# The two ends of a planned decoder kernel: another order of the first transfers and passes, small matmuls ahead of the data, and a last layer norm in 512-column pieces on VectorE

## The chip, the cores and the metric

The kernel runs on one core of a Trainium2 chip. Its time is what the device needs for one execution, in microseconds (us); the time before is the median of three executions, 1533.29 us (1532.67 to 1533.56). One further execution was taken with the hardware profiler. All rows of a profile or a trace in this text come from that one.

## The reference, cut to what matters

Two layers of a decoder trunk are computed for 512 tokens of width 1024. In each, one projection of the residual stream feeds four branches (a recurrent mixer, latent attention, a convolution, cross-attention into a memory); their outputs are merged with gates, projected once more and added to the stream, which is then normalised over its 1024 channels:

```python
for l in range(DEPTH):                       # 2
    h = x @ w_in[l]                          # cut into the inputs of all branches
    ...                                      # four branches: y_rwkv, y_mla, y_conv, y_mem
    proj = jnp.einsum('bsnc,ncd->bsnd', branches, w_o_branch[l])
    gates = jax.nn.sigmoid(merge.reshape(B, S, N_BRANCH, D) + b_gate[l])
    out = jnp.sum(gates * proj, axis=2) @ w_out[l]
    x = _layer_norm(DEEPNORM_ALPHA * x + out, ln_g[l], ln_b[l])
```

The layer norm takes mean and variance of a token's 1024 values, subtracts the one, multiplies by the reciprocal root of the other, multiplies by `ln_g` and adds `ln_b`.

## The kernel before, in words

**Arithmetic.** Every fp32 matmul is made of three passes. An operand a is split in a rounded part (called h, a cast on ScalarE) and the rest (called lo or l, a subtraction on VectorE); `mm3` then issues three matmuls: h of the left with lo of the right, h with h, lo with h. All of them go through one helper (line 322 of the profile), and every vector operation through another (line 242), so the profile tells them apart by tile names alone.

**Order.** No engine's order is left to a compiler. A planner (`Plan`) keeps a modelled clock for each engine and a modelled transfer queue, and the kernel is written as Python generators that are resumed at modelled times. Each instruction takes its place in its engine's program when its generator is resumed. All transfers are issued from SyncE's queue (SP), in the order in which the planner came to them. Some generators carry dates of their own: the transfers of x from the fifth on have the date 4000, the parameters and constants 10000, the memory tokens 24000 (modelled ns). Scratch tiles (`u`) get their places in SBUF from a first run of the same planner.

**Weights.** `stream` hands out the weight blocks in order. Two raw buffers (`WR = 2`) take the transfers; a block's raw buffer is free when both of its halves are split, and only then is the transfer of the block after next issued. `look` says how many split halves may be held in advance: 3 until the first item is done, 4 after that.

**The start.** x lies in HBM as eight slices of 128 channels by 512 tokens, 256 KB each. Before the first item the kernel issues the transfer of slice 0; `stream` then asks for the first blocks of the first projection (`w0` and `w1`, 336 KB each, two slices of channels per block); `begin` spawns the transfers of slices 1 to 7 and the splits of each slice. Besides h (`xh`) and lo (`xl`), slices 0 and 4 get a scaled fp16 copy (`xs`, made in `half_copy`), right behind their split. The first projection (`lat_item`) keeps four PSUM tiles, one per block of 128 tokens (`pl`, `pl_0x`, `pl_0xx`, `pl_0xxx`), and takes the slices k = 0 to 7 in turn: 12 matmuls of 336 columns for each k, three for each token block, with the weights' lo pass first. Slices 0 and 1 need `w0`, 2 and 3 `w1`, 4 and 5 `w2`, 6 and 7 `w3`. In the trace a weight tile carries the number of its block (w0h, w0l and so on), both halves alike; an x tile carries none.

**The end.** The last projection (`w_out` of the second layer) is computed in two halves of 512 columns. For the first half (`out_item`) all four token blocks are accumulated together; for the second (`last_item`) they come one after the other, and the last of the four in two pieces of 256 columns. `out_after` adds each PSUM result to the residual `z` and takes statistics of every 256 columns (`bn_stats`, `lbs` in the trace); behind the second half `norm` finishes a token block: `bn_aggr` (`lmv`), the reciprocal root on GpSimd (`rstd_of`: an affine step, then a power; `lrs`), a product for ScalarE's bias (`lnb`), and then, in four pieces of 256 columns, one piece by two fused steps on VectorE, three by ScalarE's affine form with product and sum by `ln_g` and `ln_b` behind it, of which GpSimd does one and VectorE two. Each piece is stored by a transfer of its own, 16 of 128 KB in all. In the second layer z is loaded and scaled in those pieces too.

Of the kernel before, what the change touches and what calls it, by code (L numbers as in the profile page):

```python
# [10 lines left out]
F32 = mybir.dt.float32  # L11
# [20 lines left out]
WS = 3  # L32
SPARE = 1024.0
RECENT = 12000.0
ALPHA = (2.0 * LAYERS) ** 0.25
KAPPA = 0.5 * math.exp(-0.5)
GN_EPS = 64e-5
# [264 lines left out]
def build(ctx: ExitStack, tc: tile.TileContext, A, out, log, slots, dbg=None):  # L302
# [26 lines left out]
    def DMA(o, i, name=None):  # L329
        n = 512  # L330
        for d in o.shape[1:]:
            n *= d
        plan.dma(n, [name] if name else _names(o), _names(i))
        plan.keep(nc.sync.dma_start(o, i))
# [50 lines left out]
    idb = cp.tile([128, 128], BF16, tag="idb", name="idb")  # L385
    bones = cp.tile([128, 128], F32R, tag="bones", name="bones")
    causal = cp.tile([128, 128], BF16, tag="causal", name="causal")
    scr = [[dp.tile([32, 256], F32, tag=f"scr{n}{i}", name=f"scr{n}{i}").rearrange("a b -> (a b)") for n in range(2)] for i in range(2)]
    zero = cp.tile([128, 64], F32, tag="zero", name="zero")
    G.memset(zero, 0.0)  # L390
# [86 lines left out]
    def weights(name, src, parts, last=False, spare=False):  # L477


        wlive["raw"] += 1  # L480
        cols = sum(parts)
        raw = wp.tile([128, 1024], F32, tag="wr", name=name, bufs=WR)[:, 0:cols]
        DMA(raw, src)
        ws = [[] for _ in parts]

        def run():
            e = 0
            for i, (w, c) in enumerate(zip(ws, parts)):
                if last:
                    h, lo = (u(f"{name}{n}{i}", 512, F32R) for n in "hl")  # L490
                else:
                    while wlive["hl"] == WH:
                        yield lambda: wlive["hl"] < WH
                    wlive["hl"] += 1
                    h = wp.tile([128, 512], F32R, tag="wh", name=f"{name}h{i}")[:, 0:c]
                    lo = wp.tile([128, 512], F32R, tag="wl", name=f"{name}l{i}")[:, 0:c]
                yield from split(h, lo, raw[:, e:e + c])
                e += c
                w.extend((h, lo))
                if spare:  # L500
                    both.add(lo.tensor.name)
                yield
            wlive["raw"] -= 1

        plan.spawn(run(), plan.done[raw.tensor.name][0])
        return ws
# [4 lines left out]
    def mm3(o, lh, ll, rh, rl, first, last):  # L511
        MM(o, lh, rl, start=first, stop=False)
        MM(o, lh, rh, start=False, stop=False)
        MM(o, ll, rh, start=False, stop=last)
# [151 lines left out]
    def half_copy(l, k, src):  # L666

        if k % 4:
            return ()
        x = xp.tile([128, 512], F16, tag="xs", name=f"xs{k}_{l}", bufs=2)  # L670
        S.activation(x, src, AF.Copy, scale=1.0 / SPARE)
        return (x,)

    def layer_items(l):
# [32 lines left out]
        def begin(get):  # L707
            if l == 0:
                def loads():
                    for k in range(1, 8):  # L710
                        if k == 4:
                            plan.t = 4000.0
                            yield
                        DMA(x0[k], A["xT"][:, k, :])
                        yield
                plan.spawn(loads())

                def splits():
                    for k in range(8):
                        plan.due(x0[k])  # L720
                        yield
                        h = xp.tile([128, 512], F32R, tag="xh", name=f"xh{k}_0")
                        lo = xp.tile([128, 512], F32R, tag="xl", name=f"xl{k}_0")
                        yield from split(h, lo, x0[k])
                        X[0].append((h, lo, *half_copy(0, k, x0[k])))

                plan.spawn(splits())
                def later():
                    yield from params(0)
                    constants()  # L730
                    plan.t = 24000.0
                    yield
                    yield from load(lambda n: u(n, 512, F32R))
                plan.spawn(later(), 10000.0)
            yield
# [533 lines left out]
        def lat_item(nb):  # L1269
            def run(get):  # L1270
                if nb == 0:
                    ps = yield from pg.take([128, 336], f"pl{nb}" + t_, 4)
                else:
                    ps = yield from pa.take([128, 336], f"pl{nb}" + t_, 2)
                    ps = [pp.tile([128, 336], F32, tag="pp", name=f"pl{nb}{i}" + t_) for i in range(2)] + ps
                for k in range(8):
                    h, lo = yield from get()
                    yield from part(X[l], k)
                    for tb in range(4):
                        xh, xl = (x[:, 128 * tb:128 * tb + 128] for x in X[l][k][:2])  # L1280
                        mm3(ps[tb], xh, xl, h, lo, k == 0, k == 7)
                        if tb % 2:
                            yield
                    free()
                if nb == 0:
                    while l and not closed[l - 1]:
                        yield lambda: closed[l - 1]
                    L["mp"] = open_phase(f"mp{l}")
                    for tb in range(4):
                        latq.append(m(f"latq{tb}" + t_, 512, "lq", 4))  # L1290
                        latk.append(m(f"latk{tb}" + t_, 512, "lk", 4))
                    L["kpe"] = m("kpe" + t_, 128, "kpe", 1)
                    L["kT"] = [tuple(m(f"kT{n}{i}" + t_, 512, f"kT{n}{i}", 1, 96, F32R) for n in "hl") for i in range(4)]
                for tb in range(4):
                    if nb == 0:
                        S.copy(latq[tb][:, 0:336], ps[tb])
                        pg.free()
                    else:
                        V.tensor_copy(latk[tb][:, 0:256], ps[tb][:, 48:304])
                        S.copy(latq[tb][:, 336:384], ps[tb][:, 0:48])  # L1300
                        S.copy(L["kpe"][:, 32 * tb:32 * tb + 32], ps[tb][:, 304:336])
                        if tb > 1:
                            pa.free()
                if nb == 1:
                    plan.spawn(latents())
                    plan.spawn(key_rotary())
                yield
            item([(A["w_lat"][l, nb, i], (336, 336)) for i in range(4)], run)
# [319 lines left out]
        E = {}  # L1628

        def end_items():  # L1630
            zn = 4 if l + 1 == LAYERS else 2
            zw = 1024 // zn

            def cut(xs, i):

# [123 lines left out]
            def store(tb, i):  # L1759
                DMA(out[:, tb, zw * i:zw * i + zw], E["z"][tb][i])  # L1760
                E["n"] += 1
                if E["n"] == 16:
                    close_phase()
                yield

# [5 lines left out]
            def norm(tb):  # L1771
                z, bs = E["z"], E["bs"][tb]
                last = l + 1 == LAYERS
                mv, rs = st(f"lmv{tb}" + t_, 2), st(f"lrs{tb}" + t_, 1)
                V.bn_aggr(mv, bs.rearrange("p (a b) -> p a b", a=4))
                rstd_of(rs, mv[:, 1:2], 1.0, 16.0 * LN_EPS)
                yield
                nb = st(f"lnb{tb}" + t_, 1)
                V.scalar_tensor_tensor(out=nb, in0=mv[:, 0:1], scalar=-1.0, in1=rs, op0=ALU.mult, op1=ALU.mult)
                if last:  # L1780
                    for i in (3, 1, 2):
                        S.activation(z[tb][i], z[tb][i], AF.Identity, scale=rs, bias=nb)
                    y, g, b = z[tb][0], cut(E["ab"][:2], 0), cut(E["ab"][2:], 0)
                    V.scalar_tensor_tensor(out=y, in0=y, scalar=mv[:, 0:1], in1=g, op0=ALU.subtract, op1=ALU.mult)
                    V.scalar_tensor_tensor(out=y, in0=y, scalar=rs, in1=b, op0=ALU.mult, op1=ALU.add)
                    plan.spawn(store(tb, 0))
                    for i, eng in ((3, G), (1, V), (2, V)):
                        y, g, b = z[tb][i], cut(E["ab"][:2], i), cut(E["ab"][2:], i)
                        eng.tensor_tensor(out=y, in0=y, in1=g, op=ALU.mult)
                        eng.tensor_tensor(out=y, in0=y, in1=b, op=ALU.add)  # L1790
                        plan.spawn(store(tb, i))
                        plan.t = plan.clk["DVE"]
                        yield
                    return
                if E["n"] == 0:
                    TOK[l + 1] = dp.tile([128, 4, 1024], F32, tag=f"x{l}", name=f"xtok{l}")
                S.activation(z[tb][0], z[tb][0], AF.Identity, scale=rs, bias=nb)
# [65 lines left out]
    def stream(items):  # L1863


        items, todo, held, runs = list(items), [], [], []
        count, look = [0], [3]

        def pick():
            for n, (blocks, run, ready, _, _) in enumerate(items):  # L1870
# [159 lines left out]
```

## Time and profile before

| what | value |
|---|---|
| median of three executions | 1533.29 us (1532.67 to 1533.56) |
| the profiled execution, its own time | 1537.36 us |
| its span, first to last instruction | 1535.5 us |
| granted TensorE clock, mean | 0.995 |
| VectorE busy | 1086.9 us (71%) |
| ScalarE busy | 703.9 us (46%) |
| GpSimd busy | 229.8 us (15%) |
| transfers, mean | 99 GB/s |

A row of the timeline gives start and length in us, engine, line of the kernel, operation, output from inputs, shapes and count, and in brackets the idle time ahead of it and what ended it. PE is TensorE, DVE VectorE, ACT ScalarE, POOL GpSimd, SPq the issuing of transfers on SyncE. A row that stands for several instructions (x7) gives the time from the first start to the last end. Lengths of consecutive matmuls overlap; the distance from start to start is what one costs.

### The profile page before, as it was taken

The numbers are of one execution on the slowest core, as the hardware profiler recorded it, in microseconds if no ns is written. First come the engines' busy times: TensorE is split into PE (matmuls) and PEld (weight loads), VectorE is DVE, ScalarE is ACT, GpSimd is POOL, SyncE is SP. The second block draws the span as 40 slices with busy tenths as digits, with TensorE's granted clock in tenths as the row PEclk, the third lists the DMA queues.
The fourth block names the chain that finished last, engine by engine and source line by source line (L and its number), as shares of the span: only waits on it lengthen the run. The fifth ranks groups of instructions, "written<-read, shape, count | busy, mean of one in ns | idle before, by whom it ended". The sixth has DMA issues, their size and how long they took to land.

```text
span 1535.5 us, 30181 instructions
## 1 busy us (share of the span) xinstructions
PE 1504.4 (98%) x11912; PEld 1233.9 (80%) x11912; DVE 1086.9 (71%) x2363; ACT 703.9 (46%) x1589; POOL 229.8 (15%) x569
## 2 busy tenths in 40 slices
PE   8999999999999999999999999999999999999997
PEld 8887788777787778888998877788777777788886
DVE  6799788988567664445555888887876777544747
ACT  5536654543444443343365465633455444433432
POOL 0000000453024310000000000000445334100002
PEclk9999999999999999999999999999999999999998
DMA  6352422212222224223343243332211231262231
GB/s 212 120 155 80 117 76 89 89 60 62 96 73 76 74 74 149 96 96 127 124 146 106 79 131 98 92 101 83 89 60 56 71 97 61 78 201 95 96 113 66
DMA packets 72141, 152.12 MB, mean 99 GB/s; under 512 B 24512, under 2 KB 30144, under 8 KB 72000
## 3 DMA queue, kind: packets, MB, share of 16 engines
q1 hardware_dynamic: 72000, 150.20, 30.9%
q8 instruction: 93, 1.52, 0.4%
q14 instruction: 48, 0.39, 0.1%
HBM read 133.39 MB, written 5.24 MB: 90 GB/s over the span
## 4 chain that ended last, share of the span: by engine, by line
PE 84%; DVE 8%; DMA 3%; ACT 3%; issue 1%; SPq 1%; POOL 0%; ACTq 0%; DVEq 0%; POOLq 0%
PE ps_m L322 21%; PE po L322 11%; PE ps_cg L322 3%; PE ps_rg L322 3%; PE ps_xg L322 3%; PE ps_v L322 3%; PE ps_xq L322 3%; PE ps_mg L322 3%; PE ps_r L322 3%; PE ps_k L322 3%; PE ms L322 2%; PE pz L322 2%; PE ps_val L322 2%; PE pl L322 2%; DMA w<-in_w_ch_dram 2%; PE ps_glu L322 2%
## 5 line engine op out<-in xcount | busy, mean ns | idle before, releaser
L242 DVE SCALAR_TENSOR_TENSOR cacc<-hpad,prm,cacc 128x512 f32<-128x512 f32 x240 | 179.1, 749 | 3.4
L242 ACT ACTIVATE tm<-ps_m,prm 128x512 f32<-128x512 f32 x64 | 44.1, 689 | 149.3 <-PE ps_m L322 135.6
L242 POOL TENSOR_SCALAR ZT<-W 32x256 f32<-32x256 f32 x16 | 10.4, 652 | 549.4 <-DMA W<-scr 319.7
L242 POOL TENSOR_TENSOR ZT<-ZT,tmpW 32x14 f32<-32x14 f32 (+6 forms) x224 | 87.9, 392 | 17.6
L242 DVE SCALAR_TENSOR_TENSOR mt<-tm,po 128x512 f32<-128x512 f32 x48 | 33.0, 687 | 78.9 <-PE po L322 68.9
L242 POOL TENSOR_TENSOR tmpW<-ZT,W 32x14 f32<-32x14 f32 (+6 forms) x224 | 83.0, 371 | 15.7
L242 POOL TENSOR_SCALAR lrs<-lmv 128x1 f32<-128x1 f32 x8 | 1.7, 207 | 353.4 <-DVE lmv L242 353.4
L242 POOL TENSOR_SCALAR gr<-gm 128x4 f32<-128x4 f32 x16 | 6.2, 388 | 251.4 <-DVE gm L242 251.4
L242 ACT ACTIVATE mP<-ms,nmm 128x128 f32<-128x128 f32 (+3 forms) x64 | 33.6, 527 | 21.8 <-DVE nmm L242 21.1
L242 ACT COPY R<-p 128x512 f32<-128x512 f32 x32 | 18.8, 586 | 38.7 <-DVE V L242 26.4
L242 DVE TENSOR_TENSOR merged<-merged,mt 128x512 f32<-128x512 f32 x48 | 33.4, 696 | 1.7
L242 ACT COPY mPT<-mt 128x128 f32<-128x128 f32 (+3 forms) x64 | 26.6, 427 | 16.8 <-PE mt L327 16.4
L242 DVE TENSOR_REDUCE nmm<-ms 128x1 f32<-128x128 f32 (+3 forms) x64 | 30.0, 484 | 0.0
L327 PE MATMUL mt<-cst,mP 128*128 128x128 f32 x160 | 27.5, 278 | 1.7 <-DVE smm L242 1.2
L242 DVE SCALAR_TENSOR_TENSOR S<-w,dpad,H 128x64 f32<-128x64 f32 x48 | 13.5, 280 | 19.9 <-PE w L322 19.9
L242 DVE TENSOR_SCALAR mP<-mP,smm 128x128 f32<-128x128 f32 (+3 forms) x64 | 24.8, 387 | 2.3
L322 PE MATMUL mo<-mPT,v 128*64 128x128 f32 x320 | 24.5, 283 | 0.0
L327 PEld LDWEIGHTS mt<-cst,mP 128*128 128x128 f32 x160 | 18.5, 141 | 7.1 <-PE ps_xg L322 1.3
L242 ACT CAST rbh<-w 128x256 fp32r<-128x256 f32 x16 | 6.5, 406 | 37.2 <-DVE w L242 37.2
L242 ACT ACTIVATE z<-z,lnb,lrs 128x256 f32<-128x256 f32 (+1 forms) x16 | 9.6, 647 | 30.3 <-DVE lnb L242 30.3
L322 PE MATMUL ms<-kTl,qT 96*128 96x128 f32 (+3 forms) x64 | 22.5, 351 | 0.1
L322 PEld LDWEIGHTS mo<-mPT,v 128*64 128x64 f32 x320 | 16.8, 136 | 6.3 <-issue 4.6
(3733 smaller groups left out, 5464.6 us busy)
## 6 DMA issues: line engine op xcount, KB each, us to landing
w<-in_w_ch_dram SPq DMA_DIRECT2D x146, 512.0 KB, 3.7
w<-in_w_o_dram SPq DMA_DIRECT2D x32, 512.0 KB, 3.8
w<-in_w_out_dram SPq DMA_DIRECT2D x16, 512.0 KB, 3.7
w<-in_w_lat_dram SPq DMA_DIRECT2D x16, 336.0 KB, 3.2
w<-in_w_mk_dram SPq DMA_DIRECT2D x8, 512.0 KB, 3.8
w<-in_w_mv_dram SPq DMA_DIRECT2D x8, 512.0 KB, 3.8
w<-in_w_qk_dram SPq DMA_DIRECT2D x8, 320.0 KB, 2.9
x<-in_xT_dram SPq DMA_DIRECT2D x8, 256.0 KB, 6.2
```

The costliest lines, as they stand in the source:

```text
L242: return self.plan.keep(f(*a, **k))
L322: plan.keep(nc.tensor.matmul(o, lhsT, rhs, start=start, stop=stop))
L327: plan.keep(nc.tensor.transpose(o, i, ident))
```

## The change

At the start:

- GpSimd clears the tile `causal` first of all, and TensorE issues 30 bf16 matmuls of 128x128 by 128x128 (`FIRST`) on it, into a PSUM tile that nobody reads.
- `look` starts at 1 in place of 3, so only `w0` is asked for before `begin` runs. The transfer of `w0` is made in two, one for each half of its columns (168 KB each). `begin` itself issues slices 1 and 2; `w1` follows, then slices 3 to 7.
- The fp16 copies of slices 0 and 4 are made after all eight splits.
- For k = 0 of the first projection the matmuls go by pass over all four token blocks, in the order xh with wh, xl with wh, xh with wl.

At the end:

- In the second layer z, residual and stores are in two pieces of 512 columns (eight stores of 256 KB) in place of four of 256.
- `norm` of the last layer adds epsilon on VectorE, leaves only the power to GpSimd, and does four fused steps of 512 columns on VectorE: (z - mean) * ln_g for both pieces, then z * rstd + ln_b for both, each followed by its store. ScalarE has no part in it, and GpSimd's product and sum and `lnb` are gone.

```diff
+FIRST = 30
@@ build
+    G.memset(causal, 0.0)
+    ps = pp.tile([128, 512], F32, tag="pp", name="first")
+    for _ in range(FIRST):
+        plan.keep(nc.tensor.matmul(ps[:, 0:128], causal, causal, start=True, stop=True))
@@ weights
-        DMA(raw, src)
+        if name == "w0":
+            DMA(raw[:, 0:parts[0]], src[:, 0:parts[0]], name)
+            DMA(raw[:, parts[0]:], src[:, parts[0]:])
+        else:
+            DMA(raw, src)
@@ begin
-                    for k in range(1, 8):
+                    plan.t = plan.now() + 1.0
+                    yield
+                    for k in range(3, 8):
                         if k == 4:
                             plan.t = 4000.0
                             yield
                         DMA(x0[k], A["xT"][:, k, :])
                         yield
+                for k in (1, 2):
+                    DMA(x0[k], A["xT"][:, k, :])
...
-                        X[0].append((h, lo, *half_copy(0, k, x0[k])))
+                        X[0].append([h, lo])
+                    for k in (0, 4):
+                        yield
+                        X[0][k].extend(half_copy(0, k, x0[k]))
@@ lat_item
+                    if l == nb == k == 0:
+                        for n, (x, w) in enumerate(((0, h), (1, h), (0, lo))):
+                            for tb in range(4):
+                                MM(ps[tb], X[l][k][x][:, 128 * tb:128 * tb + 128], w, start=n == 0, stop=False)
+                    else:
...
@@ end_items
-            zn = 4 if l + 1 == LAYERS else 2
-            zw = 1024 // zn
+            zn, zw = 2, 512
@@ norm, last layer
-                rstd_of(rs, mv[:, 1:2], 1.0, 16.0 * LN_EPS)
-                yield
-                nb = st(f"lnb{tb}" + t_, 1)
-                V.scalar_tensor_tensor(out=nb, in0=mv[:, 0:1], scalar=-1.0, in1=rs, op0=ALU.mult, op1=ALU.mult)
                 if last:
-                    for i in (3, 1, 2):
-                        S.activation(z[tb][i], z[tb][i], AF.Identity, scale=rs, bias=nb)
-                    y, g, b = z[tb][0], cut(E["ab"][:2], 0), cut(E["ab"][2:], 0)
-                    V.scalar_tensor_tensor(out=y, in0=y, scalar=mv[:, 0:1], in1=g, op0=ALU.subtract, op1=ALU.mult)
-                    V.scalar_tensor_tensor(out=y, in0=y, scalar=rs, in1=b, op0=ALU.mult, op1=ALU.add)
-                    plan.spawn(store(tb, 0))
-                    for i, eng in ((3, G), (1, V), (2, V)):
-                        y, g, b = z[tb][i], cut(E["ab"][:2], i), cut(E["ab"][2:], i)
-                        eng.tensor_tensor(out=y, in0=y, in1=g, op=ALU.mult)
-                        eng.tensor_tensor(out=y, in0=y, in1=b, op=ALU.add)
+                    V.tensor_scalar(out=rs, in0=mv[:, 1:2], scalar1=16.0 * LN_EPS, scalar2=None, op0=ALU.add)
+                    G.tensor_tensor(out=rs, in0=rs, in1=mhalf[:, 0:1], op=ALU.pow)
+                    for i in range(2):
+                        V.scalar_tensor_tensor(out=z[tb][i], in0=z[tb][i], scalar=mv[:, 0:1], in1=E["ab"][i], op0=ALU.subtract, op1=ALU.mult)
+                        plan.t = plan.clk["DVE"]
+                        yield
+                    plan.due(rs)
+                    yield
+                    for i in range(2):
+                        V.scalar_tensor_tensor(out=z[tb][i], in0=z[tb][i], scalar=rs, in1=E["ab"][2 + i], op0=ALU.mult, op1=ALU.add)
                         plan.spawn(store(tb, i))
@@ stream
-        count, look = [0], [3]
+        count, look = [0], [1]
```

More of the change, by code (lines that the diff above doesn't have):

```diff
@@ L1278, in run @@
                     yield from part(X[l], k)
[L1279 to L1282, printed above, removed]
-                            yield
+                    if l == nb == k == 0:
[3 more added lines that the diff above has]
+                    else:
+                        for tb in range(4):
+                            xh, xl = (x[:, 128 * tb:128 * tb + 128] for x in X[l][k][:2])
+                            mm3(ps[tb], xh, xl, h, lo, k == 0, k == 7)
+                            if tb % 2:
+                                yield
                     free()
@@ L1761, in store @@
                 E["n"] += 1
-                if E["n"] == 16:
+                if E["n"] == 8:
                     close_phase()
@@ L1775, in norm @@
                 V.bn_aggr(mv, bs.rearrange("p (a b) -> p a b", a=4))
+                if last:
+                    V.tensor_scalar(out=rs, in0=mv[:, 1:2], scalar1=16.0 * LN_EPS, scalar2=None, op0=ALU.add)
[5 more added lines that the diff above has]
+                    plan.due(rs)
+                    yield
+                    for i in range(2):
+                        V.scalar_tensor_tensor(out=z[tb][i], in0=z[tb][i], scalar=rs, in1=E["ab"][2 + i], op0=ALU.mult, op1=ALU.add)
+                        plan.spawn(store(tb, i))
+                        plan.t = plan.clk["DVE"]
+                        yield
+                    return
                 rstd_of(rs, mv[:, 1:2], 1.0, 16.0 * LN_EPS)
@@ L1779, in norm @@
                 V.scalar_tensor_tensor(out=nb, in0=mv[:, 0:1], scalar=-1.0, in1=rs, op0=ALU.mult, op1=ALU.mult)
-                if last:
-                    for i in (3, 1, 2):
-                        S.activation(z[tb][i], z[tb][i], AF.Identity, scale=rs, bias=nb)
-                    y, g, b = z[tb][0], cut(E["ab"][:2], 0), cut(E["ab"][2:], 0)
-                    V.scalar_tensor_tensor(out=y, in0=y, scalar=mv[:, 0:1], in1=g, op0=ALU.subtract, op1=ALU.mult)
-                    V.scalar_tensor_tensor(out=y, in0=y, scalar=rs, in1=b, op0=ALU.mult, op1=ALU.add)
-                    plan.spawn(store(tb, 0))
-                    for i, eng in ((3, G), (1, V), (2, V)):
-                        y, g, b = z[tb][i], cut(E["ab"][:2], i), cut(E["ab"][2:], i)
-                        eng.tensor_tensor(out=y, in0=y, in1=g, op=ALU.mult)
-                        eng.tensor_tensor(out=y, in0=y, in1=b, op=ALU.add)
[L1791 to L1794, printed above, removed]
                 if E["n"] == 0:
```

## The prediction

> **What bounds the kernel now.** I read the page first, then busy time by stretches, then the timeline of both ends engine by engine, and last the landing times of transfers.
>
> ```profile
> span 1535.5 us, 30181 instructions
> ...
> PE 1504.4 (98%) x11912; PEld 1233.9 (80%) x11912; DVE 1086.9 (71%) x2363; ACT 703.9 (46%) x1589; POOL 229.8 (15%) x569
> ```
>
> ```profile
> 40.00:780.00 740.00, 733.90 (x5897) 599.30 (x5897) 520.61 (x1119) 339.01 (x764) 110.75 (x273) 1.00 0.31 98
> 805.00:1500.00 695.00, 687.67 (x5503) 556.52 (x5502) 502.09 (x1088) 314.90 (x722) 107.72 (x267) 1.00 0.30 95
> ```
>
> TensorE (the second number of a stretch) bounds the kernel: 31.1 us of the span without a matmul. The two long stretches hold 6.1 and 7.3 us of that; most of the rest lies ahead of the first matmul and behind the last. The change works on those, so the most that it could save is known: 5.9 us in front and 10.3 us behind, as the next rows show. What the change alters in the middle (z of layer 2 in larger pieces, loaded and scaled on SP and DVE) lies beside a PE that is busy, and I cost it at nothing; without that cover it would still be fewer instructions than before.
>
> **The start before.**
>
> ```profile
> 3.80 0.62 ACT L242 CAST xh<-x 128x512 fp32r<-128x512 f32 x1 [1.79 <-DMA x<-in_xT_dram]
> 4.32 0.62 ACT L242 ACTIVATE xs<-x 128x512 f16<-128x512 f32 x1
> 4.86 0.45 ACT L242 CAST w0h<-w 128x336 fp32r<-128x336 f32 x1
> ...
> 10.41 0.63 ACT L242 ACTIVATE xs<-x 128x512 f16<-128x512 f32 x1
> 10.94 1.65 ACT L242 CAST xh<-x 128x512 fp32r<-128x512 f32 x3
> 12.67 0.47 ACT L242 CAST w2h<-w 128x336 fp32r<-128x336 f32 x1
> ```
>
> ```profile
> 9.61 3.86 DVE L242 TENSOR_TENSOR xl<-x,xh 128x512 fp32r<-128x512 f32 x6
> 13.39 0.50 DVE L242 TENSOR_TENSOR w2l<-w,w2h 128x336 fp32r<-128x336 f32 x1
> ```
>
> ```profile
> 5.91 0.65 PE L322 MATMUL pl<-w0l,xh 128*128 128x336 f32 x1 [5.91 <-DVE w0l L242]
> ...
> 8.31 0.48 PE L322 MATMUL pl_0xx<-w0h,xl 128*128 128x336 f32 x1
> 8.59 0.41 PE L322 MATMUL pl_0xxx<-w0l,xh 128*128 128x336 f32 x1
> ...
> 14.52 0.32 PE L322 MATMUL pl_0xxx<-w1h,xl 128*128 128x336 f32 x1
> 14.67 0.32 PE L322 MATMUL pl<-w2l,xh 128*128 128x336 f32 x1
> ```
>
> One chain leads to the first matmul: x lands, xh, the fp16 copy xs, w0h, w0l, matmul at 5.91. At first a matmul costs 0.28 us from start to start (8.31 to 8.59), later 0.15 (14.52 to 14.67). Slice k = 4, the first that uses w2, starts at 14.67.
>
> **The start after, first matmul.** xs leaves the chain: w0h follows xh at about 4.36 and ends at 4.82. w0l is now used last. So the first matmul comes at about 4.9, 1.0 us earlier. With the 0.15 us pace from there, 48 matmuls would bring k = 4 at 4.9 + 48 x 0.153 = 12.25, against 14.67: 2.4 us. I don't expect all of it, because of the transfers:
>
> ```profile
> 2.11 3.79 SPq L334 DMA_DIRECT2D x<-in_xT_dram  x7
> 7.72 2.33 SPq L334 DMA_DIRECT2D w<-in_w_lat_dram  x2
> ```
>
> ```profile
> x<-in_xT_dram SPq DMA_DIRECT2D x2, 256.0 KB, 6.6
> ```
>
> ```profile
> w<-in_w_lat_dram SPq DMA_DIRECT2D x1, 336.0 KB, 4.9
> ```
>
> The last two rows end with the time from issue to landing. The one is of the last two slices (the very last is issued at about 5.2 and lands at 11.8), the other of w2 (issued at 7.72, landing at 12.6). On SP the new order is x0, w0 in two, x1, x2, w1, x3 to x7, w2. Ahead of the end of x7 lie the same 2.7 MB as before, and the queue was never empty: x7 still lands at about 11.8, w2 at 11.8 to 12.6. Before, xh7 ended at 12.6 and w2h came at 12.67. After, ACT has the xs at 10.41 out of the way, so xh7 runs 11.8 to 12.4, w2h 12.4 to 13.1 at the latest, w2l 0.5 more: w2l is there between 13.5 and 13.65. I take 13.6, as rows for w2 lie nearest to the later one. Then k = 4 starts at 13.6 where it started at 14.67: **1.05 us gained at the start**. Nearer slices are no gate: x1 has 336 KB less ahead of it, and even if k = 1 and 2 wait some tenths, from 4.9 there are 1.35 us to spare until 13.6.
>
> Bounds. Upper: 2.4 us, if slices land sooner than before. Lower: the two moved copies stand right behind xh7 on ACT; if the planner puts both ahead of w2h (0.53 each by the distance 10.41 to 10.94), w2l comes at 14.65 and the gain is nil. By its modelled dates w2 lands between xh7 and the first copy, so I take w2h ahead. The second half of w2 stands behind both copies, but is due 1.84 us (12 matmuls) after the first.
>
> **The small matmuls.** No row shows a 128-column bf16 matmul at the slow pace. Bounds: 128/336 of 0.28 is 0.107 us, and twice that if loading the weights hides behind nothing. 30 of them take 3.2 to 6.4 us from about 1.0. In the one case TensorE is free at 4.2, ahead of the data; in the other the first real matmul waits until 6 to 7.4. Even from 6.0 at the fast pace k = 4 would come at 13.35, ahead of the 13.6 of w2l; from 7.4 at 14.7, which is the time before. I take the short end, since the page has PEld 80% busy beside a PE that is 98% busy, so loads do hide behind matmuls here. By my sum, then, these matmuls cost nothing and bring nothing: ten matmuls at 0.28 us as before, from 4.9, and 38 at 0.153 would bring k = 4 at 13.5, still ahead of w2l.
>
> The slow pace lasts from 5.91 to the matmul at 8.59, whose length is the first to shrink: 2.7 us. The Trainium skill (TensorE: Matmul & The Clock Gate, Part 1) says that the clock doubles after a busy window of about 3.4 us, that the window runs freely and that the number of slow matmuls differs from run to run. By that rule 3.2 us of small matmuls may fall just short; the sum stays as it is, and only the upper bound of 2.4 us would shrink to about 1.1.
>
> **The end before.**
>
> ```profile
> 1524.90 0.28 PE L322 MATMUL pz<-w237h,mg7l 128*128 128x256 f32 x1
> ```
>
> ```profile
> 1526.34 0.41 DVE L242 TENSOR_TENSOR z<-z,pz 128x256 f32<-128x256 f32 x1
> 1526.79 0.43 DVE L242 BATCH_NORM_STATS2 lbs<-z 128x6 f32<-128x256 f32 x1
> 1527.25 0.27 DVE L242 BATCH_NORM_AGGREGATE lmv<-lbs 128x2 f32<-128x24 f32 x1
> ...
> 1528.69 0.16 DVE L242 SCALAR_TENSOR_TENSOR lnb<-lmv,lrs 128x1 f32<-128x1 f32 x1 [0.44 <-POOL lrs L242]
> ...
> 1531.87 0.42 DVE L242 TENSOR_TENSOR z<-z,ln_b 128x256 f32<-128x256 f32 x1
> ```
>
> ```profile
> 1527.92 0.74 POOL L242 TENSOR_TENSOR lrs<-lrs,mhalf 128x1 f32<-128x1 f32 x1
> ```
>
> The last result is ready at 1525.2, but DVE takes it at 1526.34, being busy with the block before; from there it needs 5.95 us to 1532.29, and the span ends 3.2 us after that. DVE, not PE, sets this end.
>
> **The end after.**
>
> ```profile
> 62.74 0.74 DVE L242 SCALAR_TENSOR_TENSOR cacc<-hpad,prm,cacc 128x512 f32<-128x512 f32 x1
> 63.40 0.75 DVE L242 SCALAR_TENSOR_TENSOR ltl<-lt,prm,lth 128x512 fp32r<-128x512 f32 x1
> ```
>
> ```profile
> out_dram<-z SPq DMA_DIRECT2D x16, 128.0 KB, 1.9
> ...
> xtok<-z SPq DMA_DIRECT2D x8, 256.0 KB, 2.5
> ```
>
> Fused steps of 512 columns follow each other at 0.66 us and the last takes 0.75. A block of 512 columns then costs on DVE: sum 0.7 (the xl row has six two-input steps of that width in 3.86), two statistics 0.9 (0.46 from 1526.79 to the row after), aggregate 0.29, epsilon 0.1, four fused steps 3 x 0.66 + 0.75: 4.7 us. On PE such a block is 24 matmuls of 512 columns, 24 x 0.153 x 512 / 336 = 5.6 us by the pace above (an estimate), so DVE no longer falls behind. The last sum starts at 1525.25, when its data are there: 1.1 us sooner. From there sum and statistics 0.9, aggregate 0.29, epsilon 0.1, fused steps 2.73: 4.0 us to 1529.25, where it took 5.95: 1.95 us more. GpSimd's power (0.74 and some tenths of signalling) must end within the first two fused steps, 1.3 us: it fits by about 0.3. The store of 256 KB lands 0.6 later than that of 128 KB by the rows. Sum: 1.1 + 1.95 - 0.6 = **2.4 us gained at the end**. Bounds: 1.5 (power not covered, the two stores hold each other up), 3.0 (the larger store costs nothing more).
>
> For the store the skill's page DMA: Bandwidth & Descriptors (Anatomy of one DMA) has a line of 2.0 us plus size over 436 GB/s, for another path of issue; by it 128 KB more cost 0.3 us and the sum would be 2.7.
>
> **Sum.** 1.05 + 2.4 = 3.45 us. The profiled execution took 1537.36 us and would take 1533.9; its distance to the median (4.1 us) lies outside of both ends, so I subtract from the median: 1533.29 - 3.45 = 1529.8 us. A measurement of this kernel tells about 0.2%, 3.1 us, from no change; the forecast lies just beyond.
>
> **Rivals.**
>
> *No gate at the start*: the slices land sooner, and the fast pace from 4.9 is kept. For it: 1.35 us of slack and a chain that loses w1 ahead of x1. Against it: the same bytes ahead of x7. 2.4 + 2.4: 1528.5 us.
>
> *Only the end pays*: both copies ahead of w2h on ACT, or small matmuls at the long end. 1533.29 - 2.4 = 1530.9 us.
>
> *A new order eats some of it*: the planner's clock starts about 1 us earlier while its dates 4000, 10000 and 24000 stay, and scratch tiles get other places. Every later instruction may change its neighbour. What that is worth can be bounded: the two stretches quoted do the two layers in two different orders, and their idle times differ by 1.2 us. With that lost: 1531.0 to 1532 us.
>
> *Slower*: the same mechanism at another size, in the recurrent mixers, where PE waits for DVE. The two stretches hold 13.4 us of idle time. It decides from the point where this grows by half, to 20 us: then 6.7 us are lost for 3.45 gained, 1536.5 us. Only a hold-up that comes back through both layers would do that, and two orders that agree within 1.2 us speak against it.
>
> **How the numbers follow.** Forecast 0.46, no gate 0.20, only the end 0.14, order eats some 0.13, slower 0.07. Faster by over 0.2% (below 1530.2): of the forecast's 0.46, whose own range is 1528.8 to 1531.3, 0.30; of no gate 0.19; of only the end 0.03: 0.52. Slower 0.07; the rest, 0.41, within 0.2%. The range reaches from a little below no gate, 1527.7, to no change, 1533.2; beyond lie some 0.1 on each side.
>
> **What would show it.** Right: first real matmul near 4.9, k = 4 near 13.6 with PE waiting for w2l or xl just ahead; ACT without z at the end, the last sum at PE's last matmul plus 0.1, 4.0 us of DVE behind it, landing in 2.5. Wrong: k = 4 below 13 (data came sooner) or above 14.3 (copies in front); DVE waiting for lrs in the last block; idle time between the ends off by over 2 us.

## The result, and the profile after

After: 1535.74 us, median of 21 executions, against 1533.29 us for 21 of before run between them; ratio 1.0017, interval 1.0010 to 1.0023. The change makes the kernel slower by 0.17%, where 0.23% faster was forecast; the time lies outside the forecast range, 5.9 us above the forecast itself. One execution of a later kernel (e12) was slow, at 3351 us; it is left out of that kernel's ratio, and without it its median is 1529.1 us.

The profiled execution of after took 1537.66 us by its own time, 1.9 above its median; that of before 1537.36, 4.1 above its own. From the page of after, and behind it the row of the same queue from the page of before (packets, MB, share of 16 engines):

```profile
span 1535.9 us, 30159 instructions
...
PE 1505.8 (98%) x11942; PEld 1234.1 (80%) x11942; DVE 1082.1 (70%) x2330; ACT 697.9 (45%) x1577; POOL 222.0 (14%) x558
...
q8 instruction: 94, 1.54, 0.4%
```

```profile
q8 instruction: 93, 1.52, 0.4%
```

TensorE has 30 more matmuls and 30 more weight loads, and the page counts one packet more on its instruction queue, q8. What proves to matter is not this count but where the packets fall in time.

**The start.** The timeline of after, TensorE, then ScalarE, then VectorE, then SP:

```profile
0.99 3.33 PE L392 MATMUL first<-causal 128*128 128x128 bf16 x30 [0.99 <-POOL causal L243]
4.91 0.42 PE L323 MATMUL pl<-w0h,xh 128*128 128x336 f32 x1 [0.59 <-ACT w0h L243]
...
9.19 0.42 PE L323 MATMUL pl<-w0l,xh 128*128 128x336 f32 x1 [2.15 <-DVE w0l L243]
...
14.83 0.32 PE L323 MATMUL pl<-w2l,xh 128*128 128x336 f32 x1
```

```profile
7.37 0.62 ACT L243 CAST xh<-x 128x512 fp32r<-128x512 f32 x1 [2.51 <-DMA x<-in_xT_dram]
7.90 0.47 ACT L243 CAST w0h<-w 128x336 fp32r<-128x336 f32 x1
...
13.00 0.47 ACT L243 CAST w2h<-w 128x336 fp32r<-128x336 f32 x1 [0.21 <-DMA w<-in_w_lat_dram]
13.38 0.63 ACT L243 ACTIVATE xs<-x 128x512 f16<-128x512 f32 x1
```

```profile
13.67 0.50 DVE L243 TENSOR_TENSOR w2l<-w,w2h 128x336 fp32r<-128x336 f32 x1
```

```profile
9.16 2.54 SPq L335 DMA_DIRECT2D w<-in_w_lat_dram  x2
```

The first real matmul comes at 4.91, as forecast. Then TensorE stops for 2.15 us: the second half of w0 is split only behind slice 1 on ScalarE (7.90 behind 7.37), and slice 1 lands only just ahead of that. From 9.19 TensorE runs on without a gap, and k = 4 starts at 14.83, not 13.6; before it was 14.67. w0's raw buffer too comes free only with that split, so the transfer of w2 is issued at 9.16 instead of 7.72; but w2l is there at 14.17, so TensorE does not wait for it. The two fp16 copies did stay behind the first half of w2h.

**The end.** TensorE, VectorE, GpSimd, and the stores' row with their time to landing:

```profile
1527.80 0.28 PE L323 MATMUL pz<-w237h,mg7l 128*128 128x256 f32 x1
```

```profile
1528.12 0.42 DVE L243 TENSOR_TENSOR z<-z,pz 128x256 f32<-128x256 f32 x1 [0.68 <-PE pz L323]
...
1529.40 0.74 DVE L243 SCALAR_TENSOR_TENSOR z<-z,lmv,ln_g 128x512 f32<-128x512 f32 x1
1530.06 0.75 DVE L243 SCALAR_TENSOR_TENSOR z<-z,lrs,ln_b 128x512 f32<-128x512 f32 x1
1530.72 0.75 DVE L243 SCALAR_TENSOR_TENSOR z<-z,lmv,ln_g 128x512 f32<-128x512 f32 x1
1531.38 1.41 DVE L243 SCALAR_TENSOR_TENSOR z<-z,lrs,ln_b 128x512 f32<-128x512 f32 x2
```

```profile
1529.56 0.99 POOL L243 TENSOR_TENSOR lrs<-lrs,mhalf 128x1 f32<-128x1 f32 x1 [4.17 <-DVE lrs L243]
```

```profile
out_dram<-z SPq DMA_DIRECT2D x8, 256.0 KB, 2.0
```

From the last matmul's end to the end of the span it is 7.82 us (1535.9 - 1528.08), where it was 10.32: 2.50 us gained. The step at 1530.06 is block 2's last, put between the steps of block 3.

**The middle.** From k = 4 to the end of the last matmul it takes 1513.25 us (1528.08 - 14.83), before 1510.51. That is where the time came from, and in the medians it is nearer 5 us, as the profiled execution of before lies 2.2 us further above its median than that of after. The waits near 340 us show a part (total, times, longest in us), of after and then of before:

```profile
ACT w53h L243 <- DMA w<-in_w_o_dram: 4.6, 1, 4.6
...
PE ty L328 <- DVE yb L243: 2.8, 1, 2.8
DVE w53l L243 <- ACT w53h L243: 2.2, 1, 2.2
```

```profile
ACT w53h L242 <- DMA w<-in_w_o_dram: 3.2, 1, 3.2
```

A weight transfer lands later, its split on VectorE comes later, all behind that in VectorE's order too (yb among it), and TensorE waits 2.8 us for yb, as it does not at all in before. By the windows view, with the granted clock in the last column but two, it then runs a while at half pace (60 us x 0.03 / 0.5 = 3.6 us of it by the rounded clock; narrowed, the view gives a clock of 0.50 from 342.1 to 345.5 us):

```profile
300.00:360.00 60.00, 56.17 (x721) 43.16 (x720) 48.75 (x108) 28.24 (x67) 25.73 (x62) 0.97 0.25 76
```

### The profile page after: what moved, and what is told of

The parts are those of the page before. It is cut to its first block, busy times and chain, and to the rows that moved or that the text cites. A ratio compares the mean times of both kernels' runs of the same rounds, so it can differ in the third digit from the quotient of the medians.

```text
span 1535.9 us, 30159 instructions
## 1 busy us (share of the span) xinstructions
PE 1505.8 (98%) x11942; PEld 1234.1 (80%) x11942; DVE 1082.1 (70%) x2330; ACT 697.9 (45%) x1577; POOL 222.0 (14%) x558
## 4 chain that ended last, share of the span: by engine, by line
PE 82%; DVE 8%; DMA 5%; ACT 3%; issue 1%; SPq 1%; POOL 0%; DVEq 0%; ACTq 0%; POOLq 0%
PE ps_m L323 21%; PE po L323 11%; PE pz L323 4%; PE ps_cg L323 3%; PE ps_rg L323 3%; PE ps_xg L323 3%; PE ps_xq L323 3%; PE ps_v L323 3%; PE ps_mg L323 3%; PE ps_r L323 3%; PE ps_k L323 3%; PE ms L323 2%; DMA w<-in_w_ch_dram 2%; PE ps_glu L323 2%; PE ps_val L323 2%; PE p L323 1%
## 5 line engine op out<-in xcount | busy, mean ns | idle before, releaser
L243 POOL TENSOR_SCALAR ZT<-W 32x256 f32<-32x256 f32 x16 | 10.8, 675 | 552.0 <-DMA W<-scr 320.2
L243 POOL TENSOR_TENSOR lrs<-lrs,mhalf 128x1 f32<-128x1 f32 x8 | 6.4, 805 | 172.6 <-DVE lrs L243 172.2
L243 DVE SCALAR_TENSOR_TENSOR S<-w,dpad,H 128x64 f32<-128x64 f32 x48 | 13.4, 280 | 19.9 <-PE w L323 19.9
```

The lines of the kernel that those rows point to most:

```text
L243: return self.plan.keep(f(*a, **k))
```

## The experiments

Twelve kernels, in three batches of four, each batch beside executions of before on its chip. "Own" is the profiled execution's own time, to be held against the median when "k = 4" (start of that slice), "middle" and "tail" (last matmul's end to the end of the span) are read.

| kernel | median | before beside it | ratio, interval | own | k = 4 | middle | tail |
|---|---|---|---|---|---|---|---|
| before | 1533.29 | | | 1537.36 | 14.67 | 1510.51 | 10.32 |
| after | 1535.74 | 1533.29 | 1.0017 (1.0010 to 1.0023) | 1537.66 | 14.83 | 1513.25 | 7.82 |
| e1 start only | 1537.24 | 1533.10 | 1.0025 (1.0014 to 1.0036) | 1534.23 | 15.39 | 1506.87 | 10.14 |
| e2 end only | 1531.89 | 1533.10 | 0.9993 (0.9984 to 1.0002) | 1531.11 | 14.81 | 1506.33 | 7.86 |
| e3 30 small alone | 1536.98 | 1533.10 | 1.0022 (1.0011 to 1.0034) | 1537.74 | 15.08 | 1510.62 | 10.30 |
| e4 w0 first | 1537.81 | 1533.10 | 1.0030 (1.0020 to 1.0040) | 1535.57 | 14.25 | 1511.71 | 7.84 |
| e5 30 of 1 column | 1538.70 | 1533.71 | 1.0032 (1.0020 to 1.0044) | 1537.46 | 15.16 | 1510.21 | 10.23 |
| e6 8 of 512 columns | 1535.28 | 1533.71 | 1.0007 (0.9996 to 1.0018) | 1539.10 | 15.02 | 1512.03 | 10.25 |
| e7 after, none | 1531.62 | 1533.71 | 0.9986 (0.9977 to 0.9995) | 1531.47 | 15.06 | 1506.81 | 7.83 |
| e8 e7 + w0 first | 1530.35 | 1533.71 | 0.9980 (0.9969 to 0.9992) | 1530.95 | 14.50 | 1505.67 | 7.83 |
| e9 128 of 1 column | 1530.99 | 1533.19 | 0.9986 (0.9977 to 0.9994) | 1530.31 | 15.52 | 1502.73 | 10.25 |
| e10 64 of 1 column | 1540.17 | 1533.19 | 1.0043 (1.0030 to 1.0055) | 1540.17 | 15.10 | 1513.03 | 10.27 |
| e11 after, 128 of 32 | 1529.76 | 1533.19 | 0.9981 (0.9972 to 0.9990) | 1527.28 | 15.70 | 1501.77 | 7.83 |
| e12 e4, 128 of 32 | 1529.48 | 1533.19 | 0.9973 (0.9962 to 0.9984) | 1525.81 | 14.25 | 1501.98 | 7.77 |

The theories at first: A, the new order of the middle costs; B, the new end costs later on; C, a lowered clock costs. Then, for the small matmuls: I, their instructions cost; W, their work or the early full pace costs; and out of I came P, the place at which TensorE's instruction packets fall between the transfers costs.

**e1, the start alone.** The end of before put back in the kernel after:

```diff
-            zn, zw = 2, 512
+            zn = 4 if l + 1 == LAYERS else 2
...
-                    G.tensor_tensor(out=rs, in0=rs, in1=mhalf[:, 0:1], op=ALU.pow)
+                    for i in (3, 1, 2):
+                        S.activation(z[tb][i], z[tb][i], AF.Identity, scale=rs, bias=nb)
```

> The start of the change with the end of before; on every engine its instructions stand in the order of the changed kernel up to the last part of layer 2. Theory A (a new order of the middle): the whole loss is here. The start itself gains nothing (k = 4 near 14.8, as the second half of w0 is split behind slice 1), the middle takes about 2.7 us more than before, and the end gains nothing: slower than before by about 4.9 us, ratio 1.003. Theory B (the end costs): the start is even with before, ratio 1.000, and the loss comes with the end. Theory C (the clock): no fixed loss, but runs spread over 5 us, as TensorE goes slow again behind its 2.2 us gap after the first slice; ratio about 1.001 to 1.002.

**e2, the end alone.** The same lines the other way round, in the kernel before.

> The end of the change with the start of before; the order is that of before up to the last part of layer 2. Theory A: 2.4 us faster (ratio 0.9984), last matmul where it was before (1525.2), and 7.8 us from there to the end of the span where it was 10.3. Theory B: 2 us slower or more. Theory C: 2.4 us faster, spread as before.

Start alone costs 4.1 us, end alone gains 1.2 (its interval includes 1); in the profiles its tail is 2.5 shorter. B falls.

**e3, the 30 small matmuls alone**, in before. They stand outside of the planner's account, so every other instruction keeps its place on every engine (only `causal` is cleared once more by GpSimd):

```diff
+    plan.keep(nc.gpsimd.memset(causal, 0.0))
+    ps = pp.tile([128, 512], F32, tag="pp", name="first")
+    for _ in range(30):
+        plan.keep(nc.tensor.matmul(ps[:, 0:128], causal, causal, start=True, stop=True))
```

> The kernel before with the 30 small matmuls alone, kept out of the planner's account, so that every engine has the order of before. My sum: the first slice goes at 0.15 us a matmul from 5.9, but slice 1 is split at about 8.6 (xh) to 9.3 (xl), so at most 0.5 us are gained there: 0 to 0.5 us faster, ratio 0.9997 to 1.000. The clock theory: the 1.3 us that ten slow matmuls cost are all gained, ratio 0.9992, and the runs spread less.

Slower by 3.9 us, though the order is that of before. A does not explain this, and it is most of what e1 loses. Nor does C: at the same mean granted clock, 0.997, the executions of e3 have spans of 1534.2 us on average, those of before 1531.1: 3.1 of the 3.9 us are still there.

**e4, both halves of w0 split ahead of slice 1**, in after:

```diff
-                yield from split(h, lo, raw[:, e:e + c])
+                if name == "w0":
+                    for _ in split(h, lo, raw[:, e:e + c]):
+                        pass
+                else:
+                    yield from split(h, lo, raw[:, e:e + c])
...
-                yield
+                if name != "w0":
+                    yield
```

> The changed kernel, but both halves of w0 are split ahead of slice 1 on ScalarE and VectorE. In every theory slice k = 1 starts at about 8.0 in place of 9.2 and k = 4 at 13.6 in place of 14.8, as w0l of the second half no longer stands behind xh of slice 1. Theory A: the order of the middle changes again, so that of these 1.2 us anything from a gain of 3 to a loss of 2 can be left; the middle's length tells. Theory C: TensorE's gap after the first slice falls from 2.2 to about 1.1 us, the runs spread less than the 6 us of the changed kernel, and the median falls by 1.2 us or more.

k = 4 comes 0.58 us sooner (14.25), about half of the 1.2 that I expected: TensorE now waits for slice 1 itself (1.06 us for xh, up to 8.19), and w2l is there at 11.8. So the order of the splits is a part of what holds the start back, and the landing of slice 1 the other. In all the kernel is no faster than after. The loss lies elsewhere.

**e5, 30 matmuls of one column**, and **e6, 8 of 512 columns**, in before as in e3:

```diff
-    for _ in range(30):
-        plan.keep(nc.tensor.matmul(ps[:, 0:128], causal, causal, start=True, stop=True))
+    for _ in range(30):
+        plan.keep(nc.tensor.matmul(ps[:, 0:1], causal[:, 0:128], causal[:, 0:1], start=True, stop=True))
```

```diff
+    for _ in range(8):
+        plan.keep(nc.tensor.matmul(ps.rearrange("p (a b) -> p a b", a=4), causal, causal.unsqueeze(1).to_broadcast([128, 4, 128]), start=True, stop=True))
```

> The kernel before with 30 small matmuls of 1 column each ahead of its first real matmul: as many extra TensorE instructions as in the run that added the 30 matmuls of 128 columns alone (36.98 against 33.1, +0.22%), but hardly any time of work. Everything else as before. Theory I (the extra instructions cost: they shift what TensorE fetches and when against the transfers of the middle): slower by 3 to 4 us, like that run. Theory W (the work of the small matmuls costs: TensorE runs at full pace from 5 us on instead of some 8 us, and what comes after stands otherwise): within 1 us of before.

> The kernel before with 8 matmuls of 512 columns ahead of its first real matmul: about as much time of work as the 30 of 128 columns (3.3 us), but about a quarter of the instructions. Theory W: slower by 3 to 4 us, like the run with the 30 alone. Theory I: at most +1 us. If neither this nor the run with 30 of one column is slower, the loss hangs on the exact place of each instruction and not on a kind of cost.

Hardly any work but 60 instructions: +5.0 us. As much work as in e3 but 16 instructions: +1.6, with an interval that includes 1. So it is not the work; W falls.

**Where the packets fall.** The timeline shows SP's issue of the w_o transfer near 320 us, of before, e5 and after:

```profile
318.38 0.44 SPq L334 DMA_DIRECT2D w<-in_w_o_dram  x1
```

```profile
319.90 1.30 SPq L334 DMA_DIRECT2D w<-in_w_o_dram  x1
```

```profile
322.85 0.87 SPq L335 DMA_DIRECT2D w<-in_w_o_dram  x1
```

In the DMA view, cut to half a microsecond, TensorE's instruction packet starts in e5 between 319.4 and 319.9, just ahead of that issue; in before it starts between 322.0 and 322.5, about when the transfer lands. The row of e5's stretch, then the transfer's time to landing in before and in e5:

```profile
q8 instruction: 1, 0.02, 15.1%
```

```profile
w<-in_w_o_dram SPq DMA_DIRECT2D x1, 512.0 KB, 3.8
```

```profile
w<-in_w_o_dram SPq DMA_DIRECT2D x1, 512.0 KB, 4.7
```

In e1, e3 and e4 too, all with 60 more instructions, that issue takes 0.82 to 1.23 us; in e2, e6, e7 and e8, which have none or 16 more, 0.44. The second place is near 100 us. A block of w_ch and the small qT transfers behind it, in after (97 to 103.5 us, a packet among them) and in e11, an experiment below with after's order (96 to 102 us, none):

```profile
q8 instruction: 1, 0.02, 1.5%
...
w<-in_w_ch_dram SPq DMA_DIRECT2D x1, 512.0 KB, 5.4
qT<-qrh SPq DMA_DIRECT2D x2, 64.0 KB, 5.9
```

```profile
w<-in_w_ch_dram SPq DMA_DIRECT2D x2, 512.0 KB, 3.9
qT<-qrh SPq DMA_DIRECT2D x2, 64.0 KB, 3.5
```

The transfers of e11 are quicker throughout, as will be seen; e7, also with after's order and without a packet there, has 4.4 and 3.8 us in the same stretch. So the packet goes with 1.0 us more for the block and 2.1 more for qT.

Most such meetings cost little, and every kernel has many. In after a packet is under way during 59 of the 212 transfers of 512 KB, in before during 58. These land after 4.1 and 4.2 us in the median, the others after 3.7 in both, and a longer transfer is also more easily met. What counts is which transfer is met.

Why 60 instructions move it: 2 x 11912 instructions by 93 packets are 256 for each, so with 60 more in front each packet comes 60 instructions sooner in the program; here that is some 2.5 us by the clock, and some 4 us against the transfer of w_o, which e5 issues 1.5 us later than before does: from behind this transfer to just ahead of its issue.

**e7, after without small matmuls** (`FIRST = 0`), and **e8, the same with e4's edit**:

> The kernel after with the 30 small matmuls taken out, and the order of all else as it is there. If the small matmuls carry the loss (theories I and W both): the two ends are left, of which the start is even with before and the end gives 1.2 to 2.4 us, so 1531 to 1532 beside 1533.3 for before. If the new order of the middle carries it (theory A): no change to after, 1535.7, or 0.2% above before.

> The kernel after without the small matmuls and with both halves of the first weight split ahead of the second slice of x. If the small matmuls carry the loss: 0.3 to 0.9 us below the run that only leaves them out, since the fifth slice then begins some 0.6 us sooner (14.25 against 14.83 in the two runs that had the small matmuls), so about 1530.5 to 1531.5, faster than before by 0.1 to 0.2%. If the order of the middle carries it: within 1 us of after, 1535 to 1537.

Both gain: 1531.62 and 1530.35. With the same order of everything else as after, e7 is 4.1 us below it; A falls here too.

e7 also shows where in after the time goes, as both run the same 11912 matmuls in the same order behind the small ones. The matmul behind the wait for yb, in after and in e7:

```profile
340.65 0.69 PE L328 MATMUL ty<-cst,yb 128*128 128x128 f32 x2 [2.78 <-DVE yb L243]
```

```profile
334.75 0.68 PE L328 MATMUL ty<-cst,yb 128*128 128x128 f32 x2
```

At k = 4 after is 0.2 us ahead of e7. It is 2.0 us behind at the matmul that it starts at 84.44, 3.1 at the one at 108.00, 5.9 here, and 7.5 at the one at 346.02, with the stretch at half pace behind it; at the end of the last one it is 6.2, since e7 has such a stretch near 505 us. The step at 84 us belongs here too: a block of w_ch that after issues at 78.28, with a packet starting behind the issue, takes 4.9 us to landing, in e7 3.6 without a packet.

**e9 and e10, 128 and 64 matmuls of one column in before; e11, the kernel after with 128 of 32 columns; e12, the same with e4's edit.**

```diff
-FIRST = 30
+FIRST = 128
-        plan.keep(nc.tensor.matmul(ps[:, 0:128], causal, causal, start=True, stop=True))
+        plan.keep(nc.tensor.matmul(ps[:, 0:32], causal, causal[:, 0:32], start=True, stop=True))
```

> The kernel before with 128 matmuls of one column ahead of the first real one: 256 more TensorE instructions. The profile of before has 93 packets on the instruction queue (1.52 MB) for 2 x 11912 TensorE instructions, so one packet is for some 256 instructions, and this kernel's packets should stand at the same places of the program as before's, with one more at the start. Theory P (place: what costs is where an instruction packet falls between the transfers; in the run with 30 one-column matmuls two of them fell on transfers of weights, at 98 and at 320 us): within 1.5 us of before, and the transfer of w_o at some 318 us is issued in 0.44 us as there. Theory I in its plain form (each added instruction costs): 5 us for 60 instructions make some 20 for 256, at least more than that run's +5. The 128 of one column take 4.1 us at that run's 0.032 each, and so end by 5.2 us, ahead of the first data at 5.9.

> The kernel before with 64 matmuls of one column: 128 more TensorE instructions, half a packet. Theory P: the packet that stands at 322 us in before, and at 319.5 with 60 more instructions, comes some 5 us sooner than in before, at about 317, ahead of the transfer of w_o and beside two short transfers that have time; so less than 1 us is lost near 340 us; what other packets meet is not worked out, so between -1 and +4 us in all. Plain theory I: more than the +5 us of 60 instructions, some +10.

> The kernel after with 128 small matmuls of 32 columns in place of 30 of 128 columns: as much work for TensorE ahead of the first data (128 x 32 columns are 4096, 30 x 128 are 3840), but 256 extra instructions, a whole packet, instead of 60. All else in the order of after. Theory P: the loss goes, and what is left is the kernel without small matmuls (1531.6) with the first slices at full pace: 1531 to 1532. Theory W (the early work, or the early full pace, costs): 1535 to 1537, like after. Plain theory I: more than after's 1535.7, by some 10 us or more.

> The same 128 matmuls of 32 columns, with both halves of the first weight split ahead of the second slice of x: the change with both of its faults mended, if theory P holds. Theory P: 1530 to 1531, even with the run that has neither the small matmuls nor that fault (1530.35) or up to 0.3 us below, since the fifth slice began at 14.25 with small matmuls and at 14.50 without. Theory W: 1534 to 1538, like the run with 30 matmuls and this mended order (1537.8).

256 more instructions do not cost 20 us: e9 is 2.2 us *below* before, and e11, the change as given but with a whole packet of small matmuls, takes 1529.76, 6.0 us below after. e9's transfer of w_o is issued in 0.44 us again. Half a packet (e10) costs 7.0. So it is not the count. P is left, though not with my figures: e9 was to be within 1.5 us of before, e11 no faster than 1531 and e12 no faster than 1530; a whole packet more brought 1 to 2 us that P doesn't explain. The pages show that place is not all that differs in these three: their transfers land sooner throughout, met by a packet or not. The 146 blocks of w_ch, from the pages of e7 and e11:

```profile
w<-in_w_ch_dram SPq DMA_DIRECT2D x146, 512.0 KB, 3.8
```

```profile
w<-in_w_ch_dram SPq DMA_DIRECT2D x146, 512.0 KB, 3.4
```

The pages of e9 and e12 have 3.5 us, and all others, e10's among them, 3.7 or 3.8. That may well be the 1 to 2 us, though no run takes it apart, and why it is so stays open. So e9, e11 and e12 do not measure the place alone; that the small matmuls cost what after loses rests on e3, e5 and e7.

And in e10, which was to be at most 4 us slower, I moved only one packet in thought. It cleared the w_o transfer only in part (issued in 0.61 us, 4.1 to landing). The next one fell on the short store scr<-Mc (3.0 us to landing instead of 1.8), and another on w_v near 73 us. The latter's rows: e10 with the packet, e9 and before without, and TensorE's wait behind it in e10 (w_v is block w18; the half of w17 that TensorE waits for is split behind w18's first half):

```profile
q8 instruction: 1, 0.02, 0.9%
...
w<-in_w_v_dram SPq DMA_DIRECT2D x1, 512.0 KB, 6.4
```

```profile
w<-in_w_v_dram SPq DMA_DIRECT2D x1, 512.0 KB, 3.8
```

```profile
w<-in_w_v_dram SPq DMA_DIRECT2D x1, 512.0 KB, 4.6
```

```profile
78.85 0.39 PE L322 MATMUL pqe<-w17l,lth 128*128 128x256 f32 x1 [2.67 <-DVE w17l L242]
```

The kernel e12 has the lowest median, 1529.48 us, and a ratio to before of 0.9973; its distance to e11 is within the noise. k = 4 of the profile:

```profile
14.25 0.32 PE L323 MATMUL pl<-w2l,xh 128*128 128x336 f32 x1
```

## Why the prediction was wrong, step by step

- *The small matmuls "cost nothing and bring nothing".* **This step carries the error.** At the start itself it was right: 3.33 us, hidden ahead of the data. But the sum looked at nothing behind the start. There the 60 instructions moved all later packets of TensorE's program, and the middle lost more than the ends had gained: taking them out (e7) brings 4.1 us, filling them up to a whole packet (e11) 6.0, of which quicker transfers may be a part.
- *"I cost it at nothing" (the middle).* It fails only through this. The rival of a new order that eats some named the right place, idle time of TensorE between the ends, and the wrong cause: e3 and e5 lose with before's order, e7 and e11 gain with after's. The rival *slower* came near the measured time (1536.5), and one of the waits does lie in a recurrent mixer (yb), but it named the same wrong cause; TensorE's idle time in the two long stretches grew from 13.4 to 16.7 us, not to 20.
- *"Nearer slices are no gate"; 1.05 us at the start.* Wrong: slice 1 with the second half of w0 behind it on ScalarE stops TensorE for 2.15 us, so nothing is gained (14.83 against 14.67). The forecast had w2l as the gate, but TensorE waits for it in neither after nor e4. I had named k = 4 above 14.3 as the sign of copies in front; the sign came, but from slice 1. With e4's edit 14.25 was reached: 0.4 us of the 1.05.
- *The full pace from 4.9.* It held: the first matmul is 0.42 long, the next 0.32, as later on. By the Trainium skill (TensorE: Matmul & The Clock Gate, Part 1) 3.2 us of small matmuls could have fallen short of its window of about 3.4 us; in after 3.33 us did not. Since slice 1 isn't there, it brought little: k = 4 at 14.83, in e7 without them at 15.06.
- *2.4 us at the end.* Right in sum (2.50), in part by luck, with two terms off against each other. The last sum follows TensorE at once (1528.12 behind 1528.08), the 1.1 us as forecast. The chain behind it takes 4.67 us, not 4.0, since block 2's last step stands in it (0.66). The larger store was to cost 0.6 more and costs nothing: 3.1 us from VectorE's end (1532.79) to the end of the span, as against 3.2 before. Where the Trainium skill (DMA: Bandwidth & Descriptors, Anatomy of one DMA) makes it 0.3 more, the trace has 2.0 against 1.9 us to landing, 0.1. GpSimd's power stays covered, with 0.8 us to spare (1530.55 to 1531.38), of which 0.66 are that step of block 2.

What is shown: the small matmuls carry the loss, and it goes neither with how much work nor with how many instructions are added. At the places named here where the packets have moved onto transfers, the transfers land 0.3 to 2.1 us later and TensorE waits behind them.

How a packet delays a transfer is shown for w_o. The row of e5 makes 15.1% x 0.5 us x 16 = 1.2 us of one DMA engine's time for one packet. Narrowed to 0.1 us, the DMA view has it start at 319.6, so it ends at 320.8, and SyncE's issue of w_o ends 0.4 us later (319.90 + 1.30 = 321.20). The distance is 0.4 us in all six profiles in which a packet is under way at this issue: after, e1, e3, e4, e5 and e10, the last with a packet from 320.2 to 321.2 and an issue up to 321.63. So here the issue waits for the packet, and the transfer lands late by about as much or up to 0.3 us more. It isn't so for every transfer: after issues a block of w_ch at 396.95, with a packet under way, in 0.33 us.

Open: what delays w_v in e10, whose packet comes long after the issue and takes 0.9 us, where the landing is 1.8 us later than in before; and why transfers are quicker with a whole packet more.

## What to carry to other kernels

Adding instructions to an engine's program was not free here even where the engine idles: it moves where its instruction packets fall among the transfers for the whole rest of the kernel. When an edit that should be neutral costs time far away from itself, compare the times of the instruction queue's packets with the issue and landing of the transfers ahead of the new waits, and vary the count of instructions (a whole packet, half, none) before believing in the edit or against it. Look also at whether all transfers have become quicker or slower: that is another effect than the place of a packet. And a transfer that is cut in two helps only if both halves also stand ahead of the later data on the engine that converts them.

## What the runs showed of the hardware

One packet serves 256 TensorE instructions (23824 by 93), of 16 KB. The Trainium skill (Runtime: NRT & Kernel Launch, Instruction fetch mechanics) gives the same block and says that fetching it is mostly hidden. For the engine that fetches, the traces agree: the waits of TensorE quoted here all end with an operand from another engine. For the transfers they differ: what is not hidden is their delay, 3.8 to 4.7 us for w_o in e5, 4.6 to 6.4 for w_v in e10.

Small matmuls brought the full pace here only where they had columns to work on. In e9 128 matmuls of one column fill 3.57 us and the real ones begin slow (0.65 and 0.48 long); in e6 8 of 512 columns fill 3.59 us and they begin fast. TensorE's rows of e9, then of e6:

```profile
0.99 3.57 PE L391 MATMUL first<-causal 128*128 128x1 bf16 x128 [0.99 <-POOL causal L388]
6.25 0.65 PE L322 MATMUL pl<-w0l,xh 128*128 128x336 f32 x1 [1.69 <-DVE w0l L242]
6.70 0.48 PE L322 MATMUL pl<-w0h,xh 128*128 128x336 f32 x1
```

```profile
0.99 3.59 PE L391 MATMUL first<-causal 128*128 128x512 bf16 x8 [0.99 <-POOL causal L388]
6.09 0.42 PE L322 MATMUL pl<-w0l,xh 128*128 128x336 f32 x1 [1.51 <-DVE w0l L242]
6.35 0.32 PE L322 MATMUL pl<-w0h,xh 128*128 128x336 f32 x1
```

And a wait of TensorE can cost more than its length: behind the 2.8 us near 340 us in after, the granted clock is 0.50 for 3.4 us (342.1 to 345.5), 1.7 us of work lost on top.
